# An encoder layer's filter stage: Newton's steps on whole columns, low parts by ScalarE and an adding DMA, one more block of sums on VectorE

## The chip, the cores and the metric

One NeuronCore of a Trainium2 chip runs the kernel. The metric is device time in microseconds (us) of one execution; lower is better. The engines are TensorE (PE; PEld is its weight load), VectorE (DVE), ScalarE (ACT), GpSimd (POOL) and SyncE (SP), which issues DMAs.

## The reference

One layer of a bidirectional encoder on x of 1 x 1024 x 1024 in float32: an RMS norm, one input projection to 7168 columns, and two branches. The first is a diagonal state-space layer with GELU and GLU. The second, which this case is about, is a Hyena operator of order 2: two long convolutions along time. Its filters are computed from a small network:

```python
h = jnp.sin(fr * (feats @ w1 + b1))
h = jnp.sin(fr * (h @ w2 + b2))
h = h @ w3                                     # (1024 times, 4096 filters)
h = h * (jnp.exp(-t * jnp.abs(decay)) + HY_SHIFT)
k = concat([h_fwd, zeros, flip(h_bwd[1:])])    # two-sided, length 2048
k = k * lax.rsqrt(jnp.sum(k * k, axis=0) + HY_EPS)
kf = jnp.fft.rfft(k, axis=0)
```

Both branches are projected back to 1024 columns, merged by sigmoid gates, projected once more, added to x and normalised again.

## The kernel before

Products that must be more exact than one pass in the type fp32r gives are split: a value is written as a high part, rounded to fp32r, and a low part, value minus high part; three matmuls (high by high, high by low, low by high) then take the place of one. The method `split` (line 106) does this, with the high part on ScalarE (or VectorE) and the low part as a subtraction on VectorE.

The program runs in stages. First the small network (`filter_mlp`) up to its second sine. Then the filter stage (`filters`): eight units, one for each order `o` and quarter of 256 channels `cq`. Then projections, the state-space blocks, the convolutions and the output, whose matmuls fill TensorE.

A unit has two halves. `filter_time` walks over eight blocks of 128 times, in the order 4, 5, 6, 7, 0, 1, 2, 3 (`n` counts them from 0). For each block TensorE multiplies `ha` by the unit's weights `w3h` and `w3l` (lines 333, 334), ScalarE makes the decay by an exponential (336), VectorE multiplies the two into `e` (338), ScalarE squares it (342), and the forward and backward halves are added and subtracted (349, 350) into `so` (blocks 4 to 7) or `ss` and `sd` (blocks 0 to 3). These two run on VectorE for the `n` in `self.f_dve`, which is 0 and 3 (0 to 5 in the first unit), and otherwise on GpSimd. For blocks 4 to 7 `so` is split into `sh` and `sl` (line 353). GpSimd adds the squares up in `acc` (357, 362).

`filter_freq` turns the sums of a unit into its spectrum: matmuls of `sh` and `sl` (404, `po`) and of `ss` and `sd` (414, `pe`), which ScalarE and VectorE join (421 to 430) and SP stores (431). The loop in `filters` runs the time half of unit u beside the frequency half of unit u-1, in twelve steps; between them are placed the loads of the next unit's weights at step 6 (`filter_load`, whose `convert` splits `w3` at lines 316 and 317), the filter norm of unit u-1 (`filter_norm`), and a piece of `norm_in`, the norm and transposition of x (lines 457 to 480).

Both norms call `rsqrt` (line 115): a first guess by integer arithmetic (119) and three Newton steps, done for one column after another, since a per-partition scalar operand serves one column: `filter_norm` has 2 columns, `norm_in` 8.

Each engine runs its instructions in the order of its queue. The framework's scheduler fixes these orders when the program is built, from the order of the program, priorities and a model of times; `issue_after` puts a lower bound on some. Tiles with the same name share as many buffers as `bufs` says (`so` has one), and a writer waits until the readers of the buffer's previous content are done.

In the later stages `prefetch` converts the projections' weights in another way, which the change takes up:

```python
            nc.scalar.copy(out=hi, in_=raw)
            nc.scalar.activation(out=lo, in_=hi, func=AF.Copy, scale=-1.0)
            nc.gpsimd.dma_start(out=lo, in_=raw, accum_op=ALU.add)
```

ScalarE writes the negated high part into `lo`, and a DMA issued by GpSimd adds the value to it in place.

Of the kernel before, what the change touches and what calls it, by code (L numbers as in the profile page):

```python
# [9 lines left out]
F = mybir.dt.float32  # L10
# [9 lines left out]
NCH = 256  # L20
# [80 lines left out]
class Trunk:  # L101
# [4 lines left out]
    def split(self, src, hi, lo, hi_eng="act", lo_eng="dve"):  # L106
        nc = self.nc
        if hi_eng == "act":
            nc.scalar.copy(out=hi, in_=src)  # L109
        else:  # L110
            nc.vector.tensor_copy(out=hi, in_=src)  # L111
        e = nc.vector if lo_eng == "dve" else nc.gpsimd
        e.tensor_tensor(out=lo, in0=src, in1=hi, op=ALU.subtract)  # L113

    def rsqrt(self, pool, out, v, n):

        V = self.nc.vector
        h = pool.tile([128, n], F, name="rsq_h", tag="rsq_h")
        V.tensor_scalar(out=out.bitcast(I32), in0=v.bitcast(I32), scalar1=-0.5, scalar2=float(0x5F3759DF),
                        op0=ALU.mult, op1=ALU.add)  # L120
        V.tensor_scalar(out=v, in0=v, scalar1=-0.5, scalar2=None, op0=ALU.mult)
        for _ in range(3):
            for c in range(n):
                y, z = out[:, c:c + 1], h[:, c:c + 1]
                V.scalar_tensor_tensor(out=z, in0=y, scalar=v[:, c:c + 1], in1=y, op0=ALU.mult, op1=ALU.mult)
                V.scalar_tensor_tensor(out=y, in0=z, scalar=1.5, in1=y, op0=ALU.add, op1=ALU.mult)

    def reduce_2pi(self, out, x, k):
        nc = self.nc
# [113 lines left out]
    def filters(self, ctx, top):  # L243
        tc = self.tc
        c2 = ExitStack()
        mk = lambda c, n, b, **kw: c.enter_context(tc.tile_pool(name=n, bufs=b, **kw))
        self.f_dve0, self.f_dve = (0, 1, 2, 3, 4, 5), (0, 3)
        sd = [None, mk(ctx, "f_sd1", 1)]
        self.f_w = mk(ctx, "f_work", 2)
        sd[0] = mk(c2, "f_sd0", 1, side="right")  # L250
        self.f_t = mk(c2, "f_time", 2, side="right")
        self.f_pk = mk(ctx, "f_pk", 1, space=PSUM)
        self.f_px, self.f_pg = (mk(c2, n, 2, space=PSUM, side="right") for n in ("f_px", "f_pg"))
        units = [(o, cq) for o in range(2) for cq in range(4)]
        sds = {}
        x = self.norm_in()
        for u in range(len(units) + 1):
            t = iter(())
            if u < len(units):
                t = self.filter_time(*units[u], sds, sd[u % 2])  # L260
            if u == 0:
                f = self.filter_freq(*units[0], sds)
                with tc.issue_after(self.f_sin.ins):
                    for i, _ in enumerate(t):
                        if i == 2:
                            self.f_next()
                        if i == 5:
                            with tc.issue_after(self.f_g.ins):
                                self.f_turn()
                        if i > 3:  # L270
                            next(f)
                f0 = 4
                continue
            if u > 1:
                f, f0 = self.filter_freq(*units[u - 1], sds), 0
            if u == len(units):
                self.filter_norm(*units[u - 1], sds)
                c2.close()
                self.weight_pools(top)
                self.proj_pools(top)  # L280
                self.prefetch()
            for i in range(12):
                next(t, None)
                if i == 0 and u < len(units):
                    with tc.high_priority(offset=40):
                        self.filter_norm(*units[u - 1], sds)
                if i >= f0:
                    with tc.issue_after(self.f_g.ins):
                        next(f)
                if i % 3 == 0:  # L290
                    with tc.issue_after(self.f_sq.ins):
                        next(x, None)
                if i == 6 and u + 1 < len(units):
                    self.filter_load(*units[u + 1])()
            for _ in t:
                pass
            next(f, None)
        for _ in x:
            pass

    def filter_load(self, o, cq):
        nc, I = self.nc, self.I
        up, c0 = self.f_u, cq * NCH
        w3 = up.tile([128, 2, NCH], F, name="w3", bufs=1)
        src = I["hy_w3"][0].rearrange("k (x c) -> k x c", x=4)[:, 2 * o:2 * o + 2, c0:c0 + NCH]
        nc.sync.dma_start(out=w3[0:64], in_=src)
        nc.sync.dma_start(out=w3[64:128], in_=src)
        dec = up.tile([128, 2, NCH], F, name="dec")
        nc.sync.dma_start(out=dec, in_=I["hy_decay"][0].rearrange("(x c) -> x c", x=4)
                          [2 * o:2 * o + 2, c0:c0 + NCH].partition_broadcast(128))  # L310

        def convert(eng=nc.vector):
            w3h = up.tile([128, 2 * NCH], R, name="w3h")
            w3l = up.tile([128, 2 * NCH], R, name="w3l")
            w3f = w3.rearrange("k x c -> k (x c)")
            nc.scalar.copy(out=w3h, in_=w3f)
            self.f_low = eng.tensor_tensor(out=w3l, in0=w3f, in1=w3h, op=ALU.subtract)
            decf = dec.rearrange("p x c -> p (x c)")
            nc.scalar.activation(out=decf, in_=decf, func=AF.Abs)
            self.f_loaded.append((w3h, w3l, decf))  # L320
        return convert

    def filter_time(self, o, cq, sds, pool):
        nc, I = self.nc, self.I
        wp = self.f_t
        fe, fo, ha, negt = self.fc
        w3h, w3l, decf = self.f_loaded.pop(0)
        sd_t = [None] * 8
        sds[o, cq] = [sd_t, None]
        for n, tt in enumerate((4, 5, 6, 7, 0, 1, 2, 3)):  # L330
            ps = self.f_pg.tile([128, 2 * NCH], F, name="g")
            tsl = slice(tt * 128, tt * 128 + 128)
            nc.tensor.matmul(out=ps, lhsT=ha[:, tsl], rhs=w3h, start=True, stop=False)  # L333
            self.f_g = nc.tensor.matmul(out=ps, lhsT=ha[:, tsl], rhs=w3l, start=False, stop=True)
            e = wp.tile([128, 2 * NCH], F, name="e", bufs=3)
            nc.scalar.activation(out=e, in_=decf, func=AF.Exp, scale=negt[:, tt:tt + 1])
            h = e
            nc.vector.scalar_tensor_tensor(out=h, in0=e, scalar=0.05, in1=ps, op0=ALU.add, op1=ALU.mult)  # L338
            if tt == 0:
                nc.vector.memset(h[0:1, NCH:2 * NCH], 0.0)  # L340
            sq = wp.tile([128, 2 * NCH], F, name="sq" if n else "acc", bufs=2 if n else 1)
            self.f_sq = nc.scalar.activation(out=sq, in_=h, func=AF.Square)  # L342
            if tt > 3:
                so = wp.tile([128, 2, NCH], F, name="so", bufs=1)
                sd = [so[:, 0], so[:, 1]]
            else:
                sd = [pool.tile([128, NCH], F, name=f"{m}{tt}") for m in ("ss", "sd")]
            eng = nc.vector if n in (self.f_dve0 if o == cq == 0 else self.f_dve) else nc.gpsimd
            eng.tensor_tensor(out=sd[0], in0=h[:, 0:NCH], in1=h[:, NCH:], op=ALU.add)
            eng.tensor_tensor(out=sd[1], in0=h[:, 0:NCH], in1=h[:, NCH:], op=ALU.subtract)  # L350
            if tt > 3:
                hl = [pool.tile([128, 2, NCH], R, name=f"{m}{tt}") for m in ("sh", "sl")]
                self.split(so, *hl, hi_eng="dve" if o == cq == 0 and n < 4 else "act")
                sd = hl
            sd_t[tt] = sd
            if n:
                nc.gpsimd.tensor_tensor(out=acc, in0=acc, in1=sq, op=ALU.add)  # L357
            else:
                acc = sq
            sds[o, cq][1] = acc  # L360
            if n == 7:
                nc.gpsimd.tensor_tensor(out=acc[:, 0:NCH], in0=acc[:, 0:NCH], in1=acc[:, NCH:], op=ALU.add)
            yield
# [138 lines left out]
    def prefetch(self):  # L502

        nc = self.nc
        while (len(self.weights) < 2 or self.w_more) and self.order:
# [1 line left out]
            raw = self.wr.tile([128, nk, 128], F, name="wraw")  # L507
            nc.sync.dma_start(out=raw, in_=self.I[name][0, :, c * 128:c * 128 + 128].rearrange("(k p) c -> p k c", p=128))
            hi, lo = self.w_more.pop() if self.w_more else self.weight_tiles(nk)
            nc.scalar.copy(out=hi, in_=raw)  # L510
            nc.scalar.activation(out=lo, in_=hi, func=AF.Copy, scale=-1.0)  # L511
            nc.gpsimd.dma_start(out=lo, in_=raw, accum_op=ALU.add)  # L512
            self.weights.append((nxt, hi, lo))

    def weight_tiles(self, nk):
# [964 lines left out]
```

## Time and profile before

| What | us |
|---|---|
| Median of 3 runs | 1429.81 |
| Lowest and highest run | 1426.21, 1430.35 |
| Profiled execution | 1429.32 |
| Its span (first to last instruction) | 1427.5 |
| TensorE busy | 1348.4 (94%) |
| VectorE busy | 1014.9 (71%) |
| ScalarE busy | 515.0 (36%) |
| GpSimd busy | 383.6 (27%) |

The span is the stretch that the trace covers; 1.8 us of the execution lie around it. A busy share is an average over all stages. The page also cuts the span into 40 slices of 35.7 us and gives each engine's share in tenths; the filter stage fills the first seven of them:

```
PE   5888999999999999999999999999599998999997
DVE  7999997699589887314389995455389965943632
ACT  5576663232333332333332222443122215522422
POOL 3766775000000000232122200335211132432222
```

### The profile page before, as it was taken

Reading aid. Unit: us, or ns where it says so; the run is one execution under the profiler, and the core shown is the slowest. Engines: PE = TensorE matmul, PEld = TensorE weight load, DVE = VectorE, ACT = ScalarE, POOL = GpSimd, SP = SyncE. Lnnn points to the kernel's source line nnn. Section 1 sums busy time; section 2 is a strip of 40 time slices with the busy share of each in tenths; the row PEclk is TensorE's granted clock in tenths of the full one; section 3 lists DMA queues with packets and bytes.
Section 4 is the critical chain, followed back from the end, with each engine's and each line's share of the span. In section 5 each row is a group of like instructions: output and inputs, shape, how many; then the busy total and the mean of one; then the engine's idle time right before and its main releaser. Section 6 shows DMA issues by size and latency. Waiting matters only on the chain.

```text
span 1427.5 us, 19583 instructions
## 1 busy us (share of the span) xinstructions
PE 1348.4 (94%) x7219; PEld 1134.9 (80%) x7219; DVE 1014.9 (71%) x1938; ACT 515.0 (36%) x737; POOL 383.6 (27%) x331
## 2 busy tenths in 40 slices
PE   5888999999999999999999999999599998999997
PEld 3776898888888877878888888888488887978886
DVE  7999997699589887314389995455389965943632
ACT  5576663232333332333332222443122215522422
POOL 3766775000000000232122200335211132432222
PEclk9999999999999999999999999999799999999999
DMA  8222234765695544567975668865778789865431
GB/s 277 94 74 74 82 119 135 198 158 146 173 288 128 122 119 107 141 162 186 318 211 163 178 183 263 211 197 189 256 258 281 249 273 324 221 190 150 133 109 70
DMA packets 188620, 257.24 MB, mean 180 GB/s; under 512 B 23069, under 2 KB 144153, under 8 KB 185788
## 3 DMA queue, kind: packets, MB, share of 16 engines
q1 hardware_dynamic: 149212, 153.69, 34.5%
q0 software_dynamic: 11520, 39.85, 14.6%
q10 hardware_dynamic: 27792, 62.45, 12.2%
q8 instruction: 57, 0.93, 0.3%
q14 instruction: 39, 0.32, 0.1%
HBM read 147.49 MB, written 76.82 MB: 157 GB/s over the span
## 4 chain that ended last, share of the span: by engine, by line
PE 61%; DVE 17%; DMA 8%; issue 3%; ACT 1%; SPq 1%; ACTq 0%; POOL 0%; DVEq 0%
PE pps L541 39%; PE ops L1381 6%; PE iv L634 4%; PE po L404 2%; DMA zc<-c_zc_lo_d 2%; DMA d_y<-x 2%; PE fwo L685 2%; DMA yraw<-d_y 2%; PE pe L414 1%; DVE m L719 1%; PE fwe L685 1%; DVE st L1213 1%; DVE st L1211 1%; DVE e L338 1%; PE zt L670 1%
## 5 line engine op out<-in xcount | busy, mean ns | idle before, releaser
L512 POOL DMA_DIRECT2D wlo<-wraw x76 | 65.9, 867 | 685.5 <-ACT wlo L511 524.2
L541 PE MATMUL pps<-xh,whi 128*128 128x512 f32 x896 | 226.6, 401 | 3.2 <-DVE cv L565 3.2
L541 PE MATMUL pps<-xl,whi 128*128 128x512 f32 x896 | 224.1, 397 | 0.0
L541 PE MATMUL pps<-xh,wlo 128*128 128x512 f32 x896 | 222.2, 396 | 0.0
L541 PEld LDWEIGHTS pps<-xh,whi 128*128 128x128 f32 x896 | 168.0, 190 | 42.0 <-ACT wlo L511 3.6
L541 PEld LDWEIGHTS pps<-xh,wlo 128*128 128x128 f32 x896 | 166.9, 188 | 38.8
L541 PEld LDWEIGHTS pps<-xl,whi 128*128 128x128 f32 x896 | 166.3, 188 | 38.4 <-issue 0.2
L510 ACT CAST whi<-wraw 128x1024 fp32r<-128x1024 f32 (+1 forms) x76 | 74.7, 983 | 317.9 <-PE pps L541 224.1
L404 PE MATMUL po<-sh,fo 128*128 128x256 f32 x512 | 99.9, 289 | 5.9 <-DVE sh L111 5.2
L113 DVE TENSOR_TENSOR y<-yraw,y 128x512 fp32r<-128x512 f32 x64 | 58.1, 926 | 65.6 <-ACT y L109 65.5
L634 PEld LDWEIGHTS iv<-ic,y 128*128 128x128 f32 x752 | 93.6, 191 | 3.8 <-DVE y L113 2.3
L634 PE MATMUL iv<-ic,y 128*128 128x256 f32 (+1 forms) x752 | 95.3, 284 | 1.4 <-DVE y L113 1.3
L404 PEld LDWEIGHTS po<-sh,fo 128*128 128x128 f32 x512 | 82.8, 194 | 8.7 <-DVE sh L111 6.1
L511 ACT ACTIVATE wlo<-whi 128x1024 fp32r<-128x1024 f32 (+1 forms) x76 | 74.9, 986 | 27.9 <-PE pps L541 26.1
L357 POOL TENSOR_TENSOR acc<-acc,sq 128x512 f32<-128x512 f32 x56 | 75.6, 1350 | 23.2 <-ACT sq L342 22.5
L404 PE MATMUL po<-sl,fo 128*128 128x256 f32 x256 | 73.4, 287 | 1.0 <-DVE sl L113 1.0
L109 ACT CAST y<-yraw 128x512 fp32r<-128x512 f32 x64 | 39.1, 619 | 52.3 <-PE iv L634 36.6
L563 DVE SCALAR_TENSOR_TENSOR cv<-pps,cw,cv 128x1023 f32<-128x1023 f32 x24 | 30.7, 1278 | 32.2 <-ACT cv L562 32.2
L404 PEld LDWEIGHTS po<-sl,fo 128*128 128x128 f32 x256 | 49.5, 193 | 2.1 <-DVE sl L113 1.3
L685 PE MATMUL fwo<-z,zc 128*128 128x256 f32 x384 | 50.7, 285 | 0.0
L333 PE MATMUL g<-w3h,ha 128*128 128x512 f32 x64 | 33.3, 520 | 18.4 <-DVE e L338 16.7
L685 PEld LDWEIGHTS fwo<-z,zc 128*128 128x128 f32 x384 | 49.1, 194 | 1.3 <-issue 0.4
(437 smaller groups left out, 2671.4 us busy)
## 6 DMA issues: line engine op xcount, KB each, us to landing
wlo<-wraw POOLq DMA_DIRECT2D x64, 512.0 KB, 5.6
wraw<-w_in SPq DMA_DIRECT2D x56, 512.0 KB, 4.4
kspec<-ko SPq DMA_DIRECT2D x32, 512.0 KB, 3.5
kt<-kspec SPq DMA_DIRECT2D x32, 512.0 KB, 4.6
d_y<-x ACTq DMA_DIRECT2D x32, 512.0 KB, 3.9
yraw<-d_y SPq DMA_DIRECT2D x64, 256.0 KB, 6.1
d_m<-cv ACTq DMA_DIRECT2D x16, 512.0 KB, 2.7
d_z<-z ACTq DMA_DIRECT2D x8, 1024.0 KB, 5.3
```

The costliest lines, as they stand in the source:

```text
L109: nc.scalar.copy(out=hi, in_=src)
L113: e.tensor_tensor(out=lo, in0=src, in1=hi, op=ALU.subtract)
L333: nc.tensor.matmul(out=ps, lhsT=ha[:, tsl], rhs=w3h, start=True, stop=False)
L357: nc.gpsimd.tensor_tensor(out=acc, in0=acc, in1=sq, op=ALU.add)
L404: nc.tensor.matmul(out=po[:, part], lhsT=fo[a][:, 12 * (jj % 2) + b], rhs=sd[4 + i][d][:, part], start=n == 0 and part == 0, stop=n == 11 ...
L510: nc.scalar.copy(out=hi, in_=raw)
L511: nc.scalar.activation(out=lo, in_=hi, func=AF.Copy, scale=-1.0)
L512: nc.gpsimd.dma_start(out=lo, in_=raw, accum_op=ALU.add)
L541: nc.tensor.matmul(out=ps[:, hf * 512:hf * 512 + 512], lhsT=w[:, kc], rhs=part(x, kc, hf), start=a == 0 and p == 0 and kc == 0, stop=b == ...
L634: nc.tensor.matmul(out=dst, lhsT=lhsT, rhs=self.ic[b][:, j, cols], start=first, stop=last)
L685: nc.tensor.matmul(out=out, lhsT=zc[a][:, b], rhs=z[:, :, d, zi], start=start and n == 0, stop=stop and n == 3 * len(prods) - 1)
L1381: nc.tensor.matmul(out=pss[cs.start][:, 0:cs.stop - cs.start], lhsT=m[:, kc, ts], rhs=w[kc][:, cs], start=kc == 0 and p == 0, stop=kc == 7 ...
```

## The change

`rsqrt` does each Newton step on all columns at once, with three instructions a step and no scalar operand from a tile. `split` gets a third way for the low part, in place of GpSimd's subtraction: ScalarE's negated copy and the adding DMA. The filter stage uses it for `so` in all units but the first and for the filter weights `w3` in all but the first (whose low part stays on GpSimd, by `convert(nc.gpsimd)`); `prefetch` calls it with the same three instructions as before. `so` gets three buffers. In units 1 to 7 the sums of `n` = 6 (block 2) move from GpSimd to VectorE.

```diff
--- before.py
+++ after.py
@@ -109,8 +109,11 @@
             nc.scalar.copy(out=hi, in_=src)
         else:
             nc.vector.tensor_copy(out=hi, in_=src)
-        e = nc.vector if lo_eng == "dve" else nc.gpsimd
-        e.tensor_tensor(out=lo, in0=src, in1=hi, op=ALU.subtract)
+        if lo_eng == "dma":
+            nc.scalar.activation(out=lo, in_=hi, func=AF.Copy, scale=-1.0)
+            nc.gpsimd.dma_start(out=lo, in_=src, accum_op=ALU.add)
+        else:
+            nc.vector.tensor_tensor(out=lo, in0=src, in1=hi, op=ALU.subtract)
 
     def rsqrt(self, pool, out, v, n):
 
@@ -120,10 +123,9 @@
                         op0=ALU.mult, op1=ALU.add)
         V.tensor_scalar(out=v, in0=v, scalar1=-0.5, scalar2=None, op0=ALU.mult)
         for _ in range(3):
-            for c in range(n):
-                y, z = out[:, c:c + 1], h[:, c:c + 1]
-                V.scalar_tensor_tensor(out=z, in0=y, scalar=v[:, c:c + 1], in1=y, op0=ALU.mult, op1=ALU.mult)
-                V.scalar_tensor_tensor(out=y, in0=z, scalar=1.5, in1=y, op0=ALU.add, op1=ALU.mult)
+            V.tensor_tensor(out=h, in0=out, in1=out, op=ALU.mult)
+            V.tensor_tensor(out=h, in0=h, in1=v, op=ALU.mult)
+            V.scalar_tensor_tensor(out=out, in0=h, scalar=1.5, in1=out, op0=ALU.add, op1=ALU.mult)
 
     def reduce_2pi(self, out, x, k):
         nc = self.nc
@@ -244,7 +246,7 @@
         tc = self.tc
         c2 = ExitStack()
         mk = lambda c, n, b, **kw: c.enter_context(tc.tile_pool(name=n, bufs=b, **kw))
-        self.f_dve0, self.f_dve = (0, 1, 2, 3, 4, 5), (0, 3)
+        self.f_dve0, self.f_dve = (0, 1, 2, 3, 4, 5), (0, 3, 6)
         sd = [None, mk(ctx, "f_sd1", 1)]
         self.f_w = mk(ctx, "f_work", 2)
         sd[0] = mk(c2, "f_sd0", 1, side="right")
@@ -309,12 +311,15 @@
         nc.sync.dma_start(out=dec, in_=I["hy_decay"][0].rearrange("(x c) -> x c", x=4)
                           [2 * o:2 * o + 2, c0:c0 + NCH].partition_broadcast(128))
 
-        def convert(eng=nc.vector):
+        def convert(eng=None):
             w3h = up.tile([128, 2 * NCH], R, name="w3h")
             w3l = up.tile([128, 2 * NCH], R, name="w3l")
             w3f = w3.rearrange("k x c -> k (x c)")
-            nc.scalar.copy(out=w3h, in_=w3f)
-            self.f_low = eng.tensor_tensor(out=w3l, in0=w3f, in1=w3h, op=ALU.subtract)
+            if eng:
+                nc.scalar.copy(out=w3h, in_=w3f)
+                self.f_low = eng.tensor_tensor(out=w3l, in0=w3f, in1=w3h, op=ALU.subtract)
+            else:
+                self.split(w3f, w3h, w3l, lo_eng="dma")
             decf = dec.rearrange("p x c -> p (x c)")
             nc.scalar.activation(out=decf, in_=decf, func=AF.Abs)
             self.f_loaded.append((w3h, w3l, decf))
@@ -341,7 +346,7 @@
             sq = wp.tile([128, 2 * NCH], F, name="sq" if n else "acc", bufs=2 if n else 1)
             self.f_sq = nc.scalar.activation(out=sq, in_=h, func=AF.Square)
             if tt > 3:
-                so = wp.tile([128, 2, NCH], F, name="so", bufs=1)
+                so = wp.tile([128, 2, NCH], F, name="so", bufs=3)
                 sd = [so[:, 0], so[:, 1]]
             else:
                 sd = [pool.tile([128, NCH], F, name=f"{m}{tt}") for m in ("ss", "sd")]
@@ -350,7 +355,8 @@
             eng.tensor_tensor(out=sd[1], in0=h[:, 0:NCH], in1=h[:, NCH:], op=ALU.subtract)
             if tt > 3:
                 hl = [pool.tile([128, 2, NCH], R, name=f"{m}{tt}") for m in ("sh", "sl")]
-                self.split(so, *hl, hi_eng="dve" if o == cq == 0 and n < 4 else "act")
+                first = o == cq == 0
+                self.split(so, *hl, hi_eng="dve" if first else "act", lo_eng="dve" if first else "dma")
                 sd = hl
             sd_t[tt] = sd
             if n:
@@ -507,9 +513,7 @@
             raw = self.wr.tile([128, nk, 128], F, name="wraw")
             nc.sync.dma_start(out=raw, in_=self.I[name][0, :, c * 128:c * 128 + 128].rearrange("(k p) c -> p k c", p=128))
             hi, lo = self.w_more.pop() if self.w_more else self.weight_tiles(nk)
-            nc.scalar.copy(out=hi, in_=raw)
-            nc.scalar.activation(out=lo, in_=hi, func=AF.Copy, scale=-1.0)
-            nc.gpsimd.dma_start(out=lo, in_=raw, accum_op=ALU.add)
+            self.split(raw, hi, lo, lo_eng="dma")
             self.weights.append((nxt, hi, lo))
 
     def weight_tiles(self, nk):
```

## Rows read from the trace of the kernel before

**Rows 1.** Stretches: us, then busy us (x instructions) of PE, PEld, DVE, ACT, POOL; clock; DMA.
```profile
20.00:240.00 220.00, 192.11 (x1164) 167.53 (x1163) 213.13 (x455) 135.20 (x244) 150.20 (x152) 0.97 0.30 111
...
160.00:185.00 25.00, 21.99 (x143) 19.56 (x142) 23.87 (x48) 16.90 (x30) 20.78 (x20) 1.00 0.17 65
...
185.00:212.00 27.00, 26.93 (x182) 24.55 (x182) 26.90 (x54) 18.64 (x32) 19.96 (x22) 1.00 0.24 95
```

**Rows 2.** Chain that ended last: start us, us on the chain, what.
```profile
189.43 1.97 DVE rsq_h L125 x2
...
278.01 79.56 PE pps L541 x341
```

**Rows 3.** Timeline of VectorE, two neighbours: start us, us, instruction.
```profile
199.78 0.67 DVE L426 TENSOR_TENSOR ke<-pe,eo 128x512 f32<-128x512 f32 x1
200.37 0.67 DVE L338 SCALAR_TENSOR_TENSOR e<-e,g 128x512 f32<-128x512 f32 x1
```

**Rows 4.** Timeline of VectorE and GpSimd, near 161, 174 and 237 us.
```profile
160.72 1.29 POOL L357 TENSOR_TENSOR acc<-acc,sq 128x512 f32<-128x512 f32 x1 [4.99 <-ACT sq L342]
160.97 1.06 DVE L119 TENSOR_SCALAR nrm<-qs 128x2 int32<-128x2 int32 x1
...
173.65 2.17 POOL L350 TENSOR_TENSOR sd<-e 128x256 f32<-128x256 f32 x1
...
237.04 0.17 DVE L119 TENSOR_SCALAR nrm<-qs 128x2 int32<-128x2 int32 x1
237.25 0.17 DVE L121 TENSOR_SCALAR qs<-qs 128x2 f32<-128x2 f32 x1
237.45 0.35 DVE L125 SCALAR_TENSOR_TENSOR rsq_h<-nrm,qs 128x1 f32<-128x1 f32 x2
...
238.82 0.35 DVE L381 SCALAR_TENSOR_TENSOR qs<-qs,nrm,par 128x1 f32<-128x1 f32 x2
```

**Rows 5.** VectorE's groups from 20 to 240 us: count | busy us, mean ns | idle before.
```profile
L113 DVE TENSOR_TENSOR sl<-so,sh 128x512 fp32r<-128x512 f32 x32 | 24.7, 773 | 3.2 <-ACT sh L109 3.2
L125 DVE SCALAR_TENSOR_TENSOR rsq_h<-nrm,qs 128x1 f32<-128x1 f32 x48 | 20.6, 462 | 0.2
...
L350 DVE TENSOR_TENSOR so<-e 128x256 f32<-128x256 f32 x18 | 15.0, 832 | 0.0
L349 DVE TENSOR_TENSOR so<-e 128x256 f32<-128x256 f32 x17 | 12.3, 726 | 0.0
...
L126 DVE SCALAR_TENSOR_TENSOR nrm<-rsq_h,nrm 128x1 f32<-128x1 f32 x48 | 11.0, 250 | 0.0
...
L125 DVE SCALAR_TENSOR_TENSOR rsq_h<-rs,ssq 128x1 f32<-128x1 f32 x24 | 8.2, 352 | 0.0
L317 DVE TENSOR_TENSOR w3l<-w,w3h 128x512 fp32r<-128x512 f32 x7 | 6.1, 868 | 0.0
L126 DVE SCALAR_TENSOR_TENSOR rs<-rsq_h,rs 128x1 f32<-128x1 f32 x24 | 5.3, 234 | 0.0
```

**Rows 6.** GpSimd's groups from 20 to 240 us, blocks 0 to 3.
```profile
L349 POOL TENSOR_TENSOR ss<-e 128x256 f32<-128x256 f32 x30 | 26.2, 875 | 18.1 <-DVE e L338 9.5 <-DVE e L340 6.3 <-DVE rs L126 2.3
L350 POOL TENSOR_TENSOR sd<-e 128x256 f32<-128x256 f32 x30 | 25.7, 857 | 0.0
```

**Rows 7.** Later stages: a ScalarE group; line 512's DMA (ns min/median/max); its issues.
```profile
L511 ACT ACTIVATE wlo<-whi 128x512 fp32r<-128x512 f32 x12 | 7.5, 626 | 6.2 <-PE pps L541 6.2
...
L512 POOL DMA_DIRECT2D wlo<-wraw x76: 835/860/1163, 242.8 to 1309.7; - x76
...
wlo<-wraw POOLq DMA_DIRECT2D x12, 256.0 KB, 4.4
```

**Rows 8.** Waits from 20 to 235 us: who, for whom, us, times, longest.
```profile
POOL acc L357 <- ACT sq L342: 22.5, 9, 8.9
...
POOL so L349 <- DVE sl L113: 10.0, 5, 3.5
```

**Rows 9.** Tile so over the whole span: duration ns min/median/max.
```profile
L349 DVE TENSOR_TENSOR so<-e x18: 403/514/1425, 19.3 to 222.3; 128x256 f32<-128x256 f32 x18
```

## The prediction, made before the changed kernel was run

> **What bounds the kernel now.** The page's shares of busy time are averages over stages with different limits, so I went from its slices, where VectorE is full from the second on, to the view of stretches. From 20 to 240 us, the filter stage, VectorE is busy 213.1 of 220 us (97%), TensorE 192.1, GpSimd 150.2 and ScalarE 135.2 [rows 1]. TensorE's figure counts matmuls that wait in its pipe: it starts 1164 in that stretch, and 182 in the 27 us from 185 to 212; at that rate 1164 take 173 us. So VectorE sets the stage's length, and TensorE would do so only below 173 [rows 1]. The chain that ended last agrees: inside the stage it runs through VectorE, Newton's steps among it (the 1.97 us piece at 189.43), and after the stage through TensorE's projections without a gap (79.56 us from 278.01) [rows 2]. The stages behind take their weights and tiles over from the filters, so I let a shorter filter stage move all of them forward one for one. Nothing of the change lies in them: the weight conversion there is the same three instructions in a helper.
>
> One more thing must be read before the sum. VectorE instructions overlap by some 0.07 us: two neighbours of 0.67 us start 0.59 to 0.60 apart [rows 3]. So I take 0.07 off each duration. And VectorE and GpSimd hold each other up: a 128x2 operation that took 0.17 us at 237.04 took 1.06 us at 160.97, ending as GpSimd's addition of 160.72 ended; in the other direction a GpSimd subtraction whose group has a mean of 0.86 us took 2.17 us [rows 4, 6]. Mean durations of the stage contain this and I use them.
>
> **The parts.** Everything below concerns units 1 to 7 of eight; in unit 0 the low parts stay where they were, and its so buffers rise from one to three, which I cost at nothing.
> - Low parts of the sums (sl). 28 of the 32 subtractions leave VectorE: 28 x (0.773 - 0.07) = 19.7 us [rows 5]. In their place ScalarE writes the negated high part, 0.63 us for 128x512 (7.5 us for 12), and GpSimd issues an adding DMA, median 0.86 us, which lands 4.4 us after issue for 256 KB [rows 7].
> - Low parts of the filter weights (w3l). Seven more of the same: 7 x (0.868 - 0.07) = 5.6 us off VectorE [rows 5].
> - Both together put 35 x 0.63 = 22 us on ScalarE, which is busy 61% of the stage, and 35 x 0.86 = 30.1 us on GpSimd.
> - Newton's steps for the input norm (8 columns). 48 operations take 8.2 + 5.3 us, less 48 x 0.07 = 10.1 us [rows 5]. Nine remain, but each needs the one before it. The price of a dependent one stands where GpSimd is quiet: 237.04 to 237.25, 0.2 us [rows 4]. Add the delay by GpSimd, which I take from the 96 two-column operations: (20.6 + 11.0)/96 - 0.07 = 0.26 us each in the stage [rows 5] against (238.82 - 237.45)/12 = 0.11 us in quiet [rows 4], so 0.15. Nine times 0.35 is 3.2 us: 6.9 us saved.
> - Newton's steps for the filter norms (2 columns). 12 operations at 0.26 us are 3.1 us a unit; nine at 0.35 us are 3.2. The two columns had hidden each other's latency, and the fewer operations pay for that: nothing gained. Bounds: alone, 1.8 against 1.37 us, 0.43 us lost a unit, 3.4 in all; if other work fills the gaps, nine at 0.26, 0.78 gained, 6.2 in all. I take nothing, since in the stage both effects are there.
> - Sums of block 2 (the third of the three) move from GpSimd to VectorE, 14 operations. VectorE's own sums have a mean of (12.3 + 15.0)/35 = 0.78 us [rows 5], so 14 x 0.71 = 9.9 us come back on VectorE; GpSimd loses 7 x (0.875 + 0.857) = 12.1 us [rows 6].
>
> VectorE: -19.7 - 5.6 - 6.9 + 9.9 = -22.3 us. GpSimd: 150.2 - 12.1 + 30.1 = 168.2 us. Its highest share in any unit is 20.78 of 25 us, 83% [rows 1], since it waits for squares and products (22.5 us for squares alone [rows 8]); at 83% it needs 203 us, 17 less than now. So a new bound stands close to the old one, and the two give -22 and -17. I take -19, nearer GpSimd's, as its queue is in order.
>
> **New waits.** The DMA's issue waits on GpSimd for ScalarE's negated copy, and behind it queue the running sum of squares and the other sums; these free the buffers that ScalarE's squares and exponentials use, and so VectorE's products. That is why the GpSimd bound counts. The reverse goes: GpSimd waited 10.0 us for the single so buffer until the subtraction had read it [rows 8]. With three buffers it need not, though each is now held until the DMA has landed. The low part itself comes some 5 us later (0.63 + 0.86 + 4.4 against 0.70), but is read by the next unit's matmuls, half a unit or more away where a unit takes 27 us (220/8), so TensorE should not see it. SP's loads of the filter weights wait for the adding DMA instead of a subtraction, with spectrum stores behind them; the load is issued about a unit after its buffer was read, so I cost it at nothing. Without that cover it would be up to 5.3 us a unit.
>
> **A rule against it.** The adding DMAs of the later stages kept GpSimd 0.835 to 1.163 us, in stretches where it had little else to do [rows 7]; no row shows one between GpSimd's additions. The Trainium skill, "SBUF — State Buffer", section "SBUF: two separate sides", says that GpSimd cannot write the descriptors of a DMA it issues while VectorE runs an operation that takes both ports, a single-source fp32 copy inside SBUF for one. By an example of that page (620 ns alone, 3100 overlapped) an estimate for 35 issues that all meet such an operation would be 87 us more on GpSimd. By the row it is 30 us in all. In this stage VectorE mostly runs two-input operations and reads of PSUM, so I keep the row.
>
> **The time.** The profiled execution took 1429.3 us (span 1427.5 and 1.8 around it), the median of the runs is 0.5 higher. 1429.3 - 19 + 0.5 = 1411 us.
>
> **Rivals.**
> - A, the forecast (0.55): VectorE and GpSimd both near their limits, 1402 to 1420.
> - B (0.15): the full gain, with VectorE's remaining work hardly held up. Low parts 25.3, Newton 8.2 (nine at 0.21, the 8-column operation's own mean) plus 6.2, and the sums back at the least that such a sum has taken, 0.40 us [rows 9], 14 x 0.33 = 4.6: -35 us, 1395. For it: fewer two-input operations meet. Against it: GpSimd would need 91% of a 185 us stage.
> - C (0.18): GpSimd's queue takes most of it. With each issue at the largest duration seen, 1.163 us, GpSimd has 178.8 us, at 83% 215 us: -5, so 1425; between 1420 and 1429.
> - D (0.12), slower: the adding DMA's issue itself is held up, as the 2.17 us subtraction was [rows 4]. The point from which it decides: 138.1 + 35 d = 0.83 x 220, d = 1.27 us. At 1.5 us GpSimd has 190.6 us and the stage 230 us: 1439. The skill's page above is the rule for it; rows show issues below 1.27 us only, but none taken beside this stage's work.
>
> **How the numbers follow.** The sum's ends are B (1395) and C (1425); opened by a little at both ends, 1393 to 1428 leaves out D, part of C and the far tail of B, about 2 in 10. A difference under 0.3% (4.3 us) cannot be told from none. Faster: A, B and half of C, 0.79. Same: the other half of C and a little of D, 0.10. Slower: 0.11.
>
> **What would show it.** Right: in the stage VectorE's busy time falls by some 22 us and its share to 90 to 97%; GpSimd's rises to near 168 us and its share above 80%; 35 issues of adding DMAs near 0.86 us; the 8-column steps gone from ten us to about three; the stage ends 15 to 23 us earlier and every later piece of the chain shifts by as much. Wrong: issues over 1.27 us, or GpSimd waiting long for the negated copy with squares queued behind it; TensorE waiting for sl or w3l, which would name the landing; or an unchanged end with VectorE at 85%, which would name an order of work I did not see.

## The result, and the profile after

The changed kernel took 1436.39 us (median, 1434.35 to 1442.15), the kernel before beside it 1428.11 us (1426.21 to 1430.35): a ratio of 1.0057 [1.0040, 1.0073]. It is slower by 8 us, where 1411 us were forecast, and it lies outside the range.

First the stretches of the changed kernel: us, then busy us (x instructions) of PE, PEld, DVE, ACT, POOL; clock; DMA share; GB/s. The second runs from the norm of the first unit to that of the last (first `qs` instruction to first `qs` instruction).

```profile
20.00:240.00 220.00, 185.62 (x1087) 161.25 (x1085) 186.32 (x346) 151.91 (x279) 162.15 (x173) 0.92 0.52 144
...
42.50:247.20 204.70, 177.84 (x1078) 157.24 (x1079) 173.42 (x324) 140.90 (x261) 147.17 (x160) 0.92 0.48 127
```

and the second stretch in the kernel before:

```profile
45.10:236.80 191.70, 171.16 (x1065) 150.27 (x1066) 186.48 (x397) 123.50 (x225) 134.98 (x139) 0.97 0.24 89
```

VectorE is 85% busy (186.32 of 220) where it was 97% [rows 1]. From norm to norm it worked 173.4 us where the kernel before, from 45.1 to 236.8 us, needed 186.5. So 13 us of work did leave VectorE, and yet the stretch grew from 191.7 to 204.7 us: VectorE's idle time went from 5 to 31 us. TensorE's granted clock has a mean of 0.92 from 20 to 240 us, between its two levels (1.2 and 2.4 GHz, which is 1.00), where it was 0.97, and its busy time fell from 192.1 to 185.6 us; what the lower clock adds to the loss no run separates. The last matmul of `po` started at 257.5 us before and at 268.5 after; the matmuls of `tyh` (an input of a later projection), far behind the filters, started 9.9 us later (620.2, 630.1), and the span ended 10.4 us later. The loss arises in the filter stage and is carried along.

What ended VectorE's waits from norm to norm (us, times, longest), the kernel before and then the changed one:

```profile
DVE sl L113 <- ACT sh L109: 2.5, 3, 1.4
DVE ko L429 <- PE po L404: 1.5, 1, 1.5
```
```profile
DVE ko L435 <- PE po L410: 8.6, 6, 1.9
DVE e L343 <- ACT e L341: 6.6, 5, 1.6
DVE qs L381 <- PE q L377: 6.2, 2, 5.7
DVE e L343 <- PE g L339: 3.2, 2, 2.6
DVE ss L392 <- PE q L389: 2.6, 4, 0.9
```

Of the 31 us TensorE's matmuls ended some 17 (5.7 of the 6.2 us for `q` lie ahead of the stretch) and ScalarE some 9. So the loss has two faces: less work left VectorE than was forecast (13 us of 22), and VectorE waits for the two engines that feed it. The second is the larger here, and how far it follows from the first no run separates.

What answers to [rows 5] and [rows 6], groups of VectorE and GpSimd from 20 to 240 us (count | busy us, mean ns | idle before):

```profile
L354 DVE TENSOR_TENSOR ss<-e 128x256 f32<-128x256 f32 x9 | 15.5, 1722 | 0.1
L354 DVE TENSOR_TENSOR so<-e 128x256 f32<-128x256 f32 x17 | 12.3, 722 | 1.6 <-DMA sl<-so 1.5
L355 DVE TENSOR_TENSOR so<-e 128x256 f32<-128x256 f32 x18 | 11.2, 624 | 0.0
L127 DVE TENSOR_TENSOR rsq_h<-rsq_h,qs 128x2 f32<-128x2 f32 x21 | 10.7, 511 | 0.6
L128 DVE SCALAR_TENSOR_TENSOR nrm<-rsq_h,nrm 128x2 f32<-128x2 f32 x21 | 8.5, 405 | 0.6
...
L126 DVE TENSOR_TENSOR rsq_h<-nrm 128x2 f32<-128x2 f32 x21 | 6.1, 293 | 0.4
```
```profile
L114 POOL DMA_DIRECT2D sl<-so x28 | 26.9, 962 | 13.7 <-ACT sl L113 8.4 <-PE g L339 4.6 <-ACT sh L109 0.3
...
L114 POOL DMA_DIRECT2D w3l<-w x7 | 6.6, 938 | 0.0
```

The reader is to see the first line: a sum that takes 0.40 us when nothing holds it [rows 9] took 1.72 us in the mean of these nine. Two of them are unit 0's; the seven of the moved block have a mean of 2.03 us. The timeline shows why (start us, us, instruction), VectorE first, then GpSimd:

```profile
171.71 4.38 DVE L354 TENSOR_TENSOR ss<-e 128x256 f32<-128x256 f32 x1
```
```profile
171.06 0.85 POOL L114 DMA_DIRECT2D sl<-so  x1
171.66 1.55 POOL L363 TENSOR_TENSOR acc<-acc,sq 128x512 f32<-128x512 f32 x1
172.91 0.98 POOL L354 TENSOR_TENSOR ss<-e 128x256 f32<-128x256 f32 x1
173.60 0.98 POOL L355 TENSOR_TENSOR sd<-e 128x256 f32<-128x256 f32 x1
174.30 1.50 POOL L363 TENSOR_TENSOR acc<-acc,sq 128x512 f32<-128x512 f32 x1
175.51 1.11 POOL L114 DMA_DIRECT2D w3l<-w  x1
```

One VectorE sum stood for 4.38 us while GpSimd ran an issue and four additions and subtractions. Such a piece lies in the chain that ended last too (start us, us on the chain, what):

```profile
223.87 3.44 DVE rsq_h L127
```

### The profile page after: what moved, and what is told of

Read it like the earlier page. It is cut to its first block, busy times and chain, and to the rows that moved or that the text cites. A ratio compares the mean times of both kernels' runs of the same rounds, so it can differ in the third digit from the quotient of the medians.

```text
span 1437.9 us, 19654 instructions
## 1 busy us (share of the span) xinstructions
PE 1351.0 (94%) x7219; PEld 1138.4 (79%) x7219; DVE 990.3 (69%) x1854; ACT 531.6 (37%) x772; POOL 403.0 (28%) x352
## 3 DMA queue, kind: packets, MB, share of 16 engines
q0 software_dynamic: 16560, 49.03, 18.1%
## 4 chain that ended last, share of the span: by engine, by line
PE 60%; DVE 15%; DMA 9%; issue 4%; ACT 2%; POOL 1%; ACTq 0%; SPq 0%; DVEq 0%; POOLq 0%
PE pps L545 38%; PE ops L1385 5%; PE iv L638 4%; DMA d_y<-x 3%; PE po L410 3%; DMA zc<-c_zc_lo_d 2%; PE fwo L689 2%; PE pe L420 1%; DVE m L723 1%; DVE st L1217 1%; DVE st L1215 1%; PE fwe L689 1%; DVE m L722 1%; PE zt L674 1%; DMA yraw<-d_y 1%
## 5 line engine op out<-in xcount | busy, mean ns | idle before, releaser
L363 POOL TENSOR_TENSOR acc<-acc,sq 128x512 f32<-128x512 f32 x56 | 80.7, 1442 | 22.5 <-ACT sq L347 17.6
L343 DVE SCALAR_TENSOR_TENSOR e<-e,g 128x512 f32<-128x512 f32 x64 | 42.9, 676 | 12.3 <-ACT e L341 8.2
```

## The experiments

Norm to norm is the stretch from the first to the last filter norm, 191.7 us in the kernel before; "long" are single VectorE instructions over 2.0 us in it, with the sum of their durations; issues are GpSimd's DMA issues in it. Ratios are to the kernel before, with 95% intervals.

| Run | us | Ratio | Norm to norm | VectorE busy | Issues | Long |
|---|---|---|---|---|---|---|
| before | 1428.1 | | 191.7 | 186.5 | 0 | 0 |
| changed | 1436.4 | 1.0057 [1.0040, 1.0073] | 204.7 | 173.4 | 34 | 8, 22.2 us |
| e9_first_w3 | 1447.6 | 1.0117 [1.0097, 1.0137] | 200.2 | 172.1 | 33 | 7, 20.1 us |
| e1_newton | 1445.2 | 1.0095 [1.0072, 1.0117] | 202.2 | 181.4 | 0 | 0 |
| e2_lows | 1444.1 | 1.0097 [1.0079, 1.0114] | 212.9 | 168.0 | 34 | 6, 19.3 us |
| e3_sums | 1437.3 | 1.0058 [1.0038, 1.0078] | 199.9 | 192.8 | 0 | 0 |
| f1_after | 1440.1 | 1.0082 [1.0051, 1.0112] | 202.8 | 174.0 | 33 | 5, 17.3 us |
| f2_newton | 1422.4 | 0.9954 [0.9939, 0.9969] | 186.0 | 179.0 | 0 | 0 |
| f3_lows | 1443.5 | 1.0106 [1.0089, 1.0123] | 204.8 | 178.7 | 33 | 6, 19.2 us |
| f4_sums | 1436.4 | 1.0052 [1.0037, 1.0067] | 199.4 | 193.4 | 0 | 0 |
| h1_so | 1437.4 | 1.0060 [1.0045, 1.0076] | 198.0 | 183.2 | 27 | 8, 24.4 us |
| h2_w3 | 1444.5 | 1.0108 [1.0092, 1.0123] | 206.6 | 189.7 | 6 | 1, 4.7 us |
| h3_w3buf | 1435.9 | 1.0052 [1.0036, 1.0069] | 195.2 | 173.2 | 33 | 6, 19.4 us |
| h4_newton_so | 1436.3 | 1.0048 [1.0035, 1.0061] | 196.6 | 175.8 | 27 | 8, 23.6 us |
| h5_w3buf | 1435.2 | 1.0050 [1.0032, 1.0068] | 199.7 | 191.5 | 6 | 2, 7.4 us |
| n0_noacc | 1399.6 | 0.9798 [0.9780, 0.9815] | 170.7 | 159.3 | 0 | 0 |
| n1_noacc | 1409.8 | 0.9863 [0.9836, 0.9890] | 178.6 | 141.2 | 33 | 1, 2.1 us |
| d1_extra | 1458.9 | 1.0214 [1.0195, 1.0234] | 218.1 | 207.1 | 27 | 9, 29.4 us |
| d2_noissue | 1439.8 | 1.0079 [1.0060, 1.0098] | 202.5 | 191.9 | 0 | 0 |
| d3_nocopy | 1456.7 | 1.0194 [1.0174, 1.0215] | 217.1 | 203.4 | 27 | 9, 29.7 us |

**One part at a time, in the order that each kernel gets.** The changed kernel's trace showed VectorE idle before the first norm (5.74 us, waiting for the matmuls of `q`), with TensorE's low-part matmuls of unit 1 placed behind that norm. Two theories: O, this order costs; G, GpSimd's load does, by holding VectorE. e9_first_w3 is the changed kernel with unit 1's w3l on VectorE; the others are the kernel before with one part.

```diff
-                            self.f_next()
+                            self.f_next(self.nc.vector)
```

> The changed kernel with one conversion put back: the low part of the filter weights of unit 1 (the first that the change gives to the adding DMA) is again a subtraction on VectorE. Theory O (order): with the DMA the program places the low-part matmuls of unit 1's first two blocks behind the norm of unit 0 on TensorE, so VectorE sits idle until GpSimd's sum of squares, the norm and its transposes are done; that costs 9 to 12 us. Then this kernel takes 1424 to 1428 us, 8 to 12 below the changed kernel, and VectorE's idle 6 us before the first norm (36.8 to 42.5 us) is gone. Theory G (GpSimd's load): the time is lost all over the stage, through the DMA issues on GpSimd and VectorE's two-input operations that wait through runs of GpSimd's; then it takes 1432 to 1437 us.

> The kernel before with the new Newton steps alone. The forecast's terms: 6.9 us saved at the 8-column steps and nothing at the 2-column steps, if VectorE is the bound: 1421 us. Theory O and theory G both leave this part alone, so both give 1419 to 1424. If the 2-column chain of nine dependent operations costs its latency (0.4 us a unit), 1424 to 1427.

> The kernel before with the low parts by ScalarE and the adding DMA alone (so and filter weights, three so buffers), Newton's steps and the sums as before. Theory O: 25 us leave VectorE, 9 to 12 are lost at the first norm and some more to the issues on GpSimd: 1418 to 1428. Theory G: the issues on GpSimd take the whole gain and more: 1434 to 1442.

> The kernel before with the sums of the third block (n = 6) on VectorE alone. The forecast's term is 9.9 us more on VectorE, which is the bound here: 1434 to 1438. If GpSimd, relieved of 12 us, lets VectorE's other two-input operations through earlier, the two cancel: 1426 to 1431.

Newton's steps alone, forecast to save, took 14 us more than the kernel before of the same chip (1445.15 against 1431.07); e9_first_w3 became the slowest of the four, outside both theories' ranges, and e2_lows came 2 us above theory G's. Only e3_sums fell where one theory had it. In e1_newton even the stages behind the filters, where nothing is edited, lost time: the matmuls of `tyh` started 10.8 us later than before (631.0 against 620.2), those of `ozh` (a later one still) 21.2 us later (1235.3 against 1214.1). An edit of one helper gives every engine another order for the whole program, so these runs measure the part and a new order together.

**The same parts, in the order of the kernel before.** The order of the kernel before was written into the program: for each engine a list of the instructions that both kernels have, and an ordering edge without a wait from each to the next. New instructions find their own places; nine Newton steps take the first nine of the twelve old places.

```python
for a, b in zip(names, names[1:]):       # one engine's instructions, in the order of the kernel before
    tc.add_manual_dep(by[b], a, ...)     # order only, no semaphore
```

> The changed kernel, but every engine's instructions that both kernels have are held to the order in which the kernel before issues them, over the whole program; only the new instructions (ScalarE's negated copies, the adding DMAs, the sums that moved to VectorE) find their own places between. Theory S (the order that was fixed when the program was built made the loss; the parts save what the sum said): the filter stage's last po matmul comes at 238 to 248 us (before 257.5, changed 268.5) and the time is 1408 to 1418 us. Rival P (the parts themselves cost: the dependent Newton chain, VectorE held by runs of GpSimd additions, the adding DMAs): the last po matmul stays at 262 us or later and the time is 1432 us or more. Between 1420 and 1430 both share it.

> The kernel before with the new Newton steps alone, in the order of the kernel before; the same edit in its own order took 1445 us against 1431. S: 1420 to 1426 us (VectorE loses about 6.9 us of work, at some 70 to 100 per cent of it). P: 1437 us or more, because nine dependent instructions in a row stall VectorE where twelve times four filled it.

> The kernel before with the low parts by ScalarE and the adding DMA alone (three so buffers), in the order of the kernel before; in its own order 1444 us. S: 1408 to 1420 us (25 us of VectorE's work leaves; GpSimd gains 30 us of issuing at 150 of 220 us busy and may keep some of it). P: 1437 us or more.

> The kernel before with the sums of the third time block on VectorE alone, in the order of the kernel before; in its own order 1437 us. S: 1435 to 1440 us, since here the part itself puts 9.9 us of work on the engine that bounds the stage, so the order is not what made it slower. P says the same number, so this run only tells whether the parts add up: f2 + f3 + f4 against f1.

Of the two theories S is that the order made the loss, P that the parts themselves cost. Now the parts come apart. Newton's steps gain 6.1 us (1428.55 to 1422.43), as theory S had it, and 22.7 us lie between the two orders of the same program. The stretches, norm to norm, of e1_newton and of f2_newton:

```profile
46.50:248.70 202.20, 177.04 (x1071) 154.89 (x1072) 181.43 (x338) 124.66 (x226) 131.40 (x138) 0.95 0.23 84
```
```profile
46.10:232.00 185.90, 167.88 (x1065) 148.03 (x1066) 178.90 (x337) 123.28 (x225) 134.50 (x138) 0.99 0.25 91
```

Beside nearly equal work VectorE idles 20.8 us in the first and 7.0 in the second. The sums cost 7.8 us in the held order (f4_sums) and 6.3 in their own (e3_sums). The low parts cost 14.9 us in the held order too, and the whole change 11.5: for them theory S falls. The three parts' differences add up to 16.6 us, so they are not independent of each other. f2_newton is faster than both kernels.

**Which low parts, and the buffer of w.** In f3_lows SyncE waits for the adding DMAs that still read the single `w` buffer (the tile w3 in the program; line, who, us, times, longest; then its issues, start us, us):

```profile
SPq L309 <- DMA w3l<-w: 50.1, 6, 21.2
```
```profile
59.71 0.60 SPq L309 DMA_DIRECT2D w<-hy_w  x1
...
72.96 0.60 SPq L309 DMA_DIRECT2D w<-hy_w  x1
...
74.25 5.15 SPq L438 DMA_DIRECT2D kspec<-ko  x3
```

In the kernel before these two loads stood at 52.62 and 60.35 us, and the stores of the spectrum behind them at 61.66. VectorE pays, since `ko` has to be stored before its buffer comes free:

```profile
77.77 0.69 DVE L436 TENSOR_TENSOR ko<-ke,po 128x512 f32<-128x512 f32 x1 [4.51 <-DMA kspec<-ko]
```

Theory W takes this for the cost; theory H takes GpSimd's holding of VectorE. h1_so has the 28 `sl` alone, h2_w3 the `w3l` alone, h3_w3buf and h5_w3buf give `w3` a second buffer, h4_newton_so leaves the sums and `w3l` out of the change. All keep the order of the kernel before.

```diff
-        w3 = up.tile([128, 2, NCH], F, name="w3", bufs=1)
+        w3 = up.tile([128, 2, NCH], F, name="w3", bufs=2)
```

> The kernel before, in its own order, with only the 28 low parts sl by ScalarE and the adding DMA (three so buffers); the filters' low parts w3l stay on VectorE. With w3l by DMA as well it took 1443.5 us against 1428.6. Theory W (SyncE's next load of hy_w waits for the adding DMA that still reads the one w buffer, and the spectrum's stores queue behind that load, so that VectorE waits for ko's buffers): without w3l by DMA the loss goes and VectorE's saving shows, 1412 to 1426 us, and the second norm starts by 72 us. Theory H (what the subtractions gave back is taken by VectorE's other two-input instructions, which GpSimd's runs hold): 1430 to 1442 us.

> The kernel before, in its own order, with only the 7 low parts w3l by ScalarE and the adding DMA; the sl stay on VectorE. W: 1434 to 1442 us, the second norm at 76 us or later (70 before). H: 1424 to 1431 us, since seven transfers change little.

> The changed kernel held to the order of the kernel before (1440.1 us) with a second buffer for w3, so that SyncE's load need not wait for the adding DMA. W: 1424 to 1433 us, SyncE's 50.6 us of waits for w3l's DMA and VectorE's 10.3 us for the stores gone. H: 1437 to 1443 us.

> The order of the kernel before, with the new Newton steps and the 28 sl by DMA; w3l and the sums as before. By adding parts this is h1 less some 6 us. W: 1406 to 1420 us, which would beat both kernels. H: 1424 to 1436 us.

> h2_w3 (only the seven w3l by DMA, 1444.5 us) with a second w3 buffer, so that SyncE's load of hy_w need not wait for the adding DMA. If that wait is the cost: 1424 to 1434 us, and SyncE's 47 us of waits for w3l are gone. If the transfer itself is (TensorE waits for w3l): 1438 us or more.

Each alone costs: 8.9 us for the 28 `sl`, 16.0 for the `w3l`, 14.9 for both, so they don't add up. The second buffer takes SyncE's waits for `w3l` away and gives back 9.3 us where `w3l` is alone (1444.48 to 1435.15) and 4.2 in the whole change (1440.1 to 1435.9), which is within the spread of f1_after's runs. h2_w3 lies 2.5 us above W's range, h3_w3buf and h5_w3buf between the ranges of their two theories. So W is a part of the cost, and in no run all of it: without it h1_so lies where H put it, and h4_newton_so 0.3 us above H's range. In h1_so 27 subtractions of 20.2 us left the stretch, and VectorE's busy time fell by 3.3 us (186.5 to 183.2): its other instructions took most of the saving back.

**Is it the additions of GpSimd?** Both kernels in the old order, without GpSimd's 56 additions of squares (the norms are then others); the second has the whole change and the second `w3` buffer.

```diff
-            if n:
-                nc.gpsimd.tensor_tensor(out=acc, in0=acc, in1=sq, op=ALU.add)
-            else:
+            if not n:
                 acc = sq
```

> The kernel before in its own order, without GpSimd's 56 additions of squares (acc holds the first block's squares alone, so the norms are others). It is the base for n1_noacc. Both theories: 1385 to 1415 us, since some 70 us of GpSimd's 135 in the filter stage leave and VectorE's two-input instructions are held less (43.3 us for 132 Newton steps, of which about 15 are holding).

> The changed kernel in the order of the kernel before with a second w3 buffer (1435.9 us, 7.4 above the kernel before) and without the 56 additions of squares. Theory H (GpSimd's additions hold what is left of VectorE's two-input instructions and so take the saving back): the saving shows, 10 to 25 us below n0_noacc. Theory R (the way of the low parts itself is slow: copy, issue, transfer, landing): within 5 us of n0_noacc or above it.

The stretches norm to norm, n0_noacc and then n1_noacc:

```profile
37.80:208.50 170.70, 165.10 (x1065) 148.22 (x1066) 159.31 (x397) 122.67 (x225) 70.20 (x90) 0.99 0.27 100
```
```profile
38.80:217.40 178.60, 166.46 (x1065) 150.11 (x1066) 141.18 (x319) 138.29 (x258) 82.74 (x108) 0.98 0.55 144
```

VectorE's work does drop by 18.1 us here, and no long instruction but one is left; yet the time is 10 us above n0_noacc, with VectorE idle for 37 us instead of 11. That is outside H's range and in R's, but it is a weak test of H: in n0_noacc TensorE is busy 165.1 of the 170.7 us, and its 1065 matmuls at the best rate of [rows 1] (182 in 27 us) need 158, so there was little room for a saving on VectorE to show. What the run does show is that the new way can cost 10 us without long instructions. The waits in n1_noacc (us, times, longest), three of VectorE's and one of TensorE's, have other engines and transfers behind them; in n0_noacc TensorE waits for no `sl`:

```profile
DVE e L343 <- PE g L339: 10.0, 7, 2.5
DVE e L343 <- ACT e L341: 7.2, 7, 2.5
...
PE po L408 <- DMA sl<-so: 5.4, 2, 3.4
DVE ko L433 <- DMA kspec<-ko: 5.1, 5, 2.2
```

**What the added work costs by itself.** d1_extra is the kernel before, in its order, with VectorE's subtractions kept and the 28 copies and adding DMAs beside them, into a tile that nobody reads.

```diff
                 self.split(so, *hl, hi_eng="dve" if o == cq == 0 and n < 4 else "act")
+                if not o == cq == 0:
+                    dm = wp.tile([128, 2, NCH], R, name="dm", bufs=2)
+                    nc.scalar.activation(out=dm, in_=hl[0], func=AF.Copy, scale=-1.0)
+                    nc.gpsimd.dma_start(out=dm, in_=so, accum_op=ALU.add)
```

> The kernel before in its own order, VectorE's subtractions kept, and beside them 28 copies with the opposite sign on ScalarE and 28 adding DMAs into a tile that nobody reads (three so buffers, as in the change). R: 1440 us or more (the added work costs over 12 us by itself, so h1_so's +9 is its cost less what VectorE saves). H: 1427 to 1436 us (what is added is nearly free, and it is VectorE's saving that fails to show).

It costs 30.3 us (1458.88 against 1428.62), so R holds and H falls. h1_so does the same work without the 28 subtractions, at 1437.41: taking them away gave 21.5 us, near the forecast's 19.7. The two numbers are not independent: in d1_extra the subtractions that stayed had themselves grown by 8.8 us, so a part of the 21.5 is harm that only the added work does. It is the price of the way that replaced them that was wrong. Two more runs take that price apart. In d2_noissue an ordinary addition stands where each issue stood; d3_nocopy leaves out ScalarE's copies.

```diff
-                    nc.gpsimd.dma_start(out=dm, in_=so, accum_op=ALU.add)
+                    nc.gpsimd.tensor_tensor(out=dm[:, 0], in0=so[:, 0], in1=so[:, 1], op=ALU.add)
```

> d1_extra (1458.9 us) with an ordinary GpSimd addition of 128x256 (0.74 us where nothing holds it) in place of each of the 28 DMA issues (0.86 us); the 28 copies on ScalarE stay. Theory I (the issue does the harm: in the trace of d1_extra GpSimd's instructions behind an issue follow each other without a gap, each beginning 0.3 us before the end of the one before, and VectorE's two-input instructions are held through the whole run, eight of them for 27.4 us in all; the kernel before has none over 2 us): 1434 to 1446 us, and no held instruction over 2 us. Theory L (GpSimd's time alone counts): 1450 us or more.

> d1_extra without the 28 copies on ScalarE: the 28 DMAs add into two tiles that were cleared once and that nobody reads. I: 1445 to 1459 us, long holds as in d1_extra. Theory C (the copies in ScalarE's chain of exp, square and high part cost): 1430 to 1442 us.

Leaving out the copies gave 2.2 us (1458.88 to 1456.67), within the intervals of the two runs; theory C falls. An addition in place of the issue costs 11.2 us in all, and the issue with its transfer 19.0 us more than it, though both occupy GpSimd for about the same time: means of 0.84 and 0.86 us. The same place in both, d1_extra first, VectorE's sum and then GpSimd:

```profile
57.23 4.02 DVE L349 TENSOR_TENSOR so<-e 128x256 f32<-128x256 f32 x1
```
```profile
56.23 0.86 POOL L357 DMA_DIRECT2D dm<-so  x1 [1.09 <-issue]
56.84 1.56 POOL L361 TENSOR_TENSOR acc<-acc,sq 128x512 f32<-128x512 f32 x1
58.07 0.99 POOL L349 TENSOR_TENSOR ss<-e 128x256 f32<-128x256 f32 x1
58.75 0.99 POOL L350 TENSOR_TENSOR sd<-e 128x256 f32<-128x256 f32 x1
59.43 1.53 POOL L361 TENSOR_TENSOR acc<-acc,sq 128x512 f32<-128x512 f32 x1
```

and d2_noissue:

```profile
58.41 0.58 DVE L349 TENSOR_TENSOR so<-e 128x256 f32<-128x256 f32 x1
58.92 0.94 DVE L350 TENSOR_TENSOR so<-e 128x256 f32<-128x256 f32 x1
```
```profile
56.30 1.71 POOL L361 TENSOR_TENSOR acc<-acc,sq 128x512 f32<-128x512 f32 x1
57.98 0.73 POOL L357 TENSOR_TENSOR dm<-so 128x256 fp32r<-128x256 f32 x1
58.68 0.90 POOL L349 TENSOR_TENSOR ss<-e 128x256 f32<-128x256 f32 x1
59.54 0.91 POOL L350 TENSOR_TENSOR sd<-e 128x256 f32<-128x256 f32 x1
60.41 1.28 POOL L361 TENSOR_TENSOR acc<-acc,sq 128x512 f32<-128x512 f32 x1
```

Behind the issue GpSimd's starts follow at 1.23, 0.68 and 0.68 us, and VectorE's sum gets its turn only when the run of four is over, at 60.96. Behind the ordinary addition VectorE's two sums get in after one GpSimd instruction each, and GpSimd gives way in turn: its start steps are 0.70, 0.86 and 0.87 us. Over the whole stretch the same instructions of VectorE were busy 207.1 us in d1_extra, 191.9 in d2_noissue and 186.5 in the kernel before. That is 15.2 us more with the issues, of the 15.6 by which the two stretches differ, and in d1_extra no engine waits for one of the added transfers in the stretch. Theory I stands: it is VectorE's held instructions that make the difference. In the table no kernel without an issue in the stretch has a long instruction, and every kernel with 27 or more issues beside the full additions has five to nine (d1_extra nine, where the expectation of d2_noissue counted eight).

## Why the prediction was wrong

- **What bounds the kernel: right for the kernel before.** VectorE's work sets its stage: f2_newton took 6.9 us by the forecast's working and gave 6.1, f4_sums put 9.9 us on VectorE and cost 7.8, and the 28 subtractions, put at 19.7 us, gave 21.5 once the added work was in both kernels (with the caution above).
- **Newton's steps: right in size**, but only in the order of the kernel before and by themselves: beside the 28 `sl` by DMA they gave 1.2 us (h1_so 1437.4, h4_newton_so 1436.3). In the order that the framework gave the same edit it cost 14 us. That step, that an edit leaves the order around it as it was, was taken silently and failed. For the whole change the order is not the cause: 1440.1 us in the old order, 1436.4 in its own. The eight-column steps went to 3.0 us (1.7 + 0.9 + 0.4 in the groups of the three lines), as forecast.
- **The low parts: the step that failed.** "By the row it is 30 us in all. In this stage VectorE mostly runs two-input operations and reads of PSUM, so I keep the row." The row priced GpSimd's time for an issue, and nearly rightly: means of 0.96 and 0.94 us here, 0.86 taken. What an issue does to VectorE was put at nothing. For the 28 `sl`, against 21.5 us saved stand 30.3: 19.0 for the issues with their transfers, beyond an ordinary GpSimd instruction of that length, and 11.2 for that much more work among GpSimd's additions together with the copies. The instructions that stayed on VectorE paid it.
- **The sums of block 2: mis-sized by the same step.** The 14 moved operations took 20.3 us in the changed kernel and 10.1 in f4_sums, which issues no DMA there. The sum took VectorE's mean for such an operation, 0.78 us, from a stage without issues.
- **"GpSimd at 83%" was the wrong bound.** GpSimd was busy 162.2 of 220 us, 74%, and VectorE 85%; neither was near its limit. An engine's busy time at an earlier kernel's best share did not bound a stage in which the engines wait for each other.
- **SyncE's loads: "I cost it at nothing" failed**, but the uncovered price of up to 5.3 us a unit was far too much: the second buffer gave back 9.3 us in all for `w3l` alone, 1.3 a unit, and 4.2 in the whole change in the old order. In the changed kernel's own order SyncE waits 20.2 us for `w3l` in two waits; there the second buffer was not tried.
- **The rule on the page.** The Trainium skill, "SBUF — State Buffer", section "SBUF: two separate sides", has GpSimd locked out while VectorE runs an operation that takes both ports, and its issues late. That direction hardly shows: 28 issues of `sl` had a median of 0.859 us, the longest 1.877. The same section says that of a VectorE operation with two inputs in SBUF and a GpSimd operation that reads SBUF, whichever starts first has the port pair "for the whole instruction", the other being blocked; the matched timelines agree for d2_noissue. In d1_extra VectorE's sum stood through the run of GpSimd's instructions behind the issue, not through one alone.
- **Rivals.** D had the sign and nearly the size (1439), but by another mechanism: the issues had a mean of 0.96 us, under its 1.27, and two of the 28 were over that. That it came near is luck. Of the signs, TensorE's wait for `sl` is small here (3.1 us in four waits) and 5.4 us in n1_noacc. The last sentence of the forecast names VectorE at 85%, which the profile shows, and an unchanged end, which came 11 us later; what it takes for the cause, the order, does not explain it, since the old order gave no better time.

What stays open: how the changed kernel's 8 us divide, since the holding of VectorE was priced for the 28 `sl` in the kernel before and most of VectorE's loss here is waiting; why n1_noacc, with hardly a long instruction, is still 10 us above n0_noacc (VectorE waits there for `g`, for ScalarE's exponentials and for transfers, TensorE for `sl`; which of them starts the loss was not separated); where the later stages of e1_newton lose their 10 us; and whether an issue placed where GpSimd goes idle next would spare VectorE. That last was not tried.

## What to carry to other kernels

Before an issue of a DMA goes to GpSimd's queue, look at who shares time with GpSimd in that stage: between GpSimd's additions and VectorE's two-input work, 28 issues cost 30 us with their copies and transfers, where the row from a quiet stage said that they would be covered. Price a moved operation by adding its replacement and keeping the original (d1_extra); beside the run without the original it sets the cost against the saving. And where a scheduler orders the program, measure a part in the old order as well: the same Newton steps gave -6 us in one and +14 in the other.

## What the runs showed of the hardware that was not expected

- Behind a DMA issue GpSimd's additions follow each other while a VectorE instruction stands: for up to 4.38 us in the changed kernel (seven of its eight long ones stand in such a run) and 5.2 us in d1_extra (a subtraction at 244.78 us; all its nine do), against a maximum of 1.84 us in the kernels that issue no DMA there. Why an issue has this effect the profile does not show.
- The instructions that were left as they were pay: the 27 `sl` of VectorE from norm to norm have a mean of 749 ns in the kernel before and 1074 ns in d1_extra, 8.8 us of the 26.4 that the stretch grew by:

```profile
L113 DVE TENSOR_TENSOR sl<-so,sh 128x512 fp32r<-128x512 f32 x27 | 20.2, 749 | 2.5 <-ACT sh L109 2.5
...
L113 DVE TENSOR_TENSOR sl<-so,sh 128x512 fp32r<-128x512 f32 x27 | 29.0, 1074 | 2.4 <-ACT sh L109 2.3
```

- Without GpSimd's 56 accumulations the same instructions of VectorE took 159.3 us instead of 186.5: 27 us of VectorE's busy time in the kernel before goes with them.
